# Chunked linear attention inside a long fp32 kernel: scores' full blocks ahead of their corners, the scaling split and moved, a copy on another engine

## The chip, the core and the metric

One core of a Trainium2 chip runs the whole kernel. Its engines take their instructions in order, each from its own queue: TensorE (PE in the profile; its weight loads stand as PEld), VectorE (DVE), ScalarE (ACT), GpSimd (POOL) and SyncE (SP, which issues DMAs). They wait for each other by semaphores. The metric is the device time of one execution in microseconds; lower is better.

## The reference

One block of a model: two gated feed-forward parts around a mixer, on 512 positions of width 1024, in fp32. The change touches the mixer's chunked linear attention, four heads of key width 128 and value width 256, in chunks of 64 positions.

```
b = jnp.cumsum(gc, axis=3)
q_ref = qc * jnp.exp(b - b_ref)
k_ref = kc * jnp.exp(b_ref - b)
scores = jnp.where(causal, jnp.einsum('bhnid,bhnjd->bhnij', q_ref, k_ref), 0.0)
o_intra = jnp.einsum('bhnij,bhnjv->bhniv', scores, vc)
q_inter = q_ref * jnp.exp(b_ref)
k_state = kc * jnp.exp(b_last - b)
kv = jnp.einsum('bhncd,bhncv->nbhdv', k_state, vc)
def step(state, inp):
    dec, kv_n = inp
    return state * dec[..., None] + kv_n, state
o = o_intra + o_inter
```

## The kernel before

**Projections.** Weights come by DMA in fp32. Each is split into a high half `wh` (a cast on ScalarE, L391) and a low half `wl` (a subtraction on VectorE, L392), and each product is taken as three matmuls: high by high, high by low of the activations, low by high. The three buffers of `wh` and of `wl` let this run two units ahead of TensorE. Most projections go by a scheme of seven products (steps m1, p2, q6, p5, q7, p3, p4). The projections v, ga and gb (`Tall`, matmuls at L702) have two halves to each step, 12 matmuls a half; in "ga, p4, second half" the second half of the weights is meant. The ones behind them (`Set`, L586) are numbered from 0 and take 24 matmuls a step. A finished step is evacuated by ScalarE (L1353) or VectorE (L1355). Some sums of weights are made by DMAs of GpSimd's queue that add into a buffer (L360), and by VectorE (L370, L385).

**Attention.** The four heads are worked between the steps of these projections. A table (`hooks`) names, for each step, the pieces that are recorded right behind it. A scheduler then orders each engine's instructions, mostly as they were recorded. A head goes through these pieces:

- `gates` (L1221 to L1230): one matmul, then an absolute value, an exponential and a logarithm on ScalarE (L1224, L1227, L1228), a sum of two on VectorE (L1229) and the running sum along a chunk (a scan, L1230) into tile E.
- `decays` (L1235 to L1245): two differences on VectorE, five exponentials on ScalarE.
- `scale`: nine multiplications on VectorE, all of line L557 (`mul`). Six make the scaled q and k and the tiles KX, QX and KS that scores and state need; three make QS and d2s, which only state and output need.
- `scores`: for each of four blocks of 128 positions (two chunks) a full block (L1272, weights of 128 columns, 128x128) and a corner (L1273, weights of 64 columns, 64x64), which writes a quarter of that full block's place with other scaling; then a masked copy on VectorE (L1275), and three transposes of KS (L1284), copied by ScalarE (L1285).
- `state`: three matmuls (L1294). The first and second write the two halves of one PSUM bank, the third another bank. The first result is copied to the state tile (L1297, VectorE), the others are added to the decayed state before (L1299).
- `output` and `squares`: the two parts of the result (L1313, L1316), and the sum of squares for its norm.

Two PSUM banks (`aux`) serve these pieces in turn.

Of the kernel before, what the change touches and what calls it, by code (L numbers as in the profile page):

```python
# [27 lines left out]
NTB = S // P  # L28
# [192 lines left out]
def block_kernel(ctx: ExitStack, tc: tile.TileContext, xT, vecs, gf, gup, wgl, wts, out):  # L221
    nc = tc.nc
# [37 lines left out]
    def tile_of(pool, shape, dtype=F32):  # L260
        cnt[0] += 1
        return pools[pool].tile(shape, dtype, tag=pool, name=f"{pool}{cnt[0]}")
# [12 lines left out]
    def AUX():  # L275
        cnt[0] += 1
        return pa.tile([P, S], F32, tag="aux", name=f"aux{cnt[0]}")
# [189 lines left out]
    def split(v):  # L467
        h = T(F32R)
        l = T(F32R)
        nc.scalar.copy(h, v)  # L470
        nc.vector.tensor_tensor(out=l, in0=v, in1=h.bitcast(F32), op=ALU.subtract)
        return h, l
# [83 lines left out]
    def mul(out_, a, b, eng=None):  # L556
        (eng or nc.vector).tensor_tensor(out=out_, in0=a, in1=b, op=ALU.mult)  # L557
# [533 lines left out]
    def mixer(norm, nxt):  # L1091
# [15 lines left out]
        def two(i):  # L1107
            return flat(i).rearrange("p (e t) -> p e t", e=2)

        QK = [two(0), two(1)] + [tile_of("qk", [P, 2, S]) for _ in range(2)]  # L1110
# [95 lines left out]
        def pairs(t):  # L1206
            return t.rearrange("p (b e t) -> p b e t", e=2, t=CH)
# [5 lines left out]
        sm4 = sm.rearrange("p a (b e) -> p a b e", e=2)  # L1213
        d2s = cpool.tile([P, NTB], F32, tag="d2", name="d2")
        ST = [M[:, :DV], M[:, DV:], stt2]
        vs = cpool.tile([P, 16 * HEADS], F32, tag="vs", name="vs")

        def gates(h):

            a = AUX()  # L1220
            nc.tensor.matmul(a, gup_w[:R3, h * DK : (h + 1) * DK], glr[:R3],  # L1221
                             start=True, stop=True)
            b = vec[:, V_GB + h : V_GB + h + 1]
            nc.scalar.activation(E, a, AF.Abs, bias=b)  # L1224
            nc.vector.tensor_scalar(out=M, in0=a, scalar1=b, scalar2=0.0,
                                    op0=ALU.add, op1=ALU.min)
            nc.scalar.activation(E, E, AF.Exp, scale=-1.0)  # L1227
            nc.scalar.activation(E, E, AF.Ln, bias=1.0)  # L1228
            nc.vector.tensor_tensor(out=M, in0=M, in1=E, op=ALU.subtract)  # L1229
            nc.vector.tensor_tensor_scan(out=E, data0=reset, data1=M, initial=0.0,  # L1230
                                         op0=ALU.mult, op1=ALU.add)
# [15 lines left out]
        def bc(t):  # L1247
            return t.unsqueeze(2).to_broadcast([P, NTB, CH])

        def scale(h):  # L1250

            q_, k_ = QK[h][:, 0], QK[h][:, 1]
            ref, dc = sm4[:, 0], sm4[:, 1]
            mul(q_, EX, q_)
            mul(KX, pairs(KS)[:, :, 0], pairs(k_)[:, :, 0])
            mul(QX, pairs(q_)[:, :, 1], bc(ref[:, :, 1]))
            mul(pairs(KS)[:, :, 1], pairs(KS)[:, :, 1], pairs(k_)[:, :, 1])
            mul(k_, M, k_)  # L1260
            mul(pairs(KS)[:, :, 0], KX, bc(dc[:, :, 1]))
            mul(pairs(QS)[:, :, 1], QX, bc(dc[:, :, 0]))
            mul(pairs(QS)[:, :, 0], pairs(q_)[:, :, 0], bc(ref[:, :, 0]))
            mul(d2s, dc[:, :, 0], dc[:, :, 1])

        def scores(h):

            q_, k_ = QK[h][:, 0], QK[h][:, 1]
            st = AUX()
            for t in range(NTB):  # L1270
                b = slice(t * P, (t + 1) * P)
                nc.tensor.matmul(st[:, b], k_[:, b], q_[:, b], start=True, stop=True)  # L1272
                nc.tensor.matmul(st[:CH, t * P + CH : (t + 1) * P], KX[:, t], QX[:, t],  # L1273
                                 start=True, stop=True)
            nc.vector.copy_predicated(  # L1275
                sc.rearrange("p (b i) -> p b i", i=P),
                mask.unsqueeze(1).to_broadcast([P, NTB, P]),
                st.rearrange("p (b i) -> p b i", i=P),
            )
            n = NTB - 1  # L1280
            tr = AUX()
            for t in range(n):
                b = slice(t * P, (t + 1) * P)
                nc.tensor.transpose(tr[:, b], KS[:, b], ident)  # L1284
            nc.scalar.copy(E[:, : n * P], tr[:, : n * P])  # L1285

        def state(h):

            v = vt[h // 2]
            for t in range(NTB - 1):  # L1290
                if t % 2 == 0:
                    kv = AUX()
                hc = slice((t % 2) * DV, (t % 2) * DV + DV)
                nc.tensor.matmul(kv[:, hc], E[:, t * P : (t + 1) * P],  # L1294
                                 v[t][:, (h % 2) * DV : (h % 2) * DV + DV], start=True, stop=True)
                if t == 0:
                    nc.vector.tensor_copy(ST[0], kv[:, hc])  # L1297
                else:
                    nc.vector.scalar_tensor_tensor(out=ST[t], in0=ST[t - 1],  # L1299
                                                   scalar=d2s[:, t : t + 1], in1=kv[:, hc],  # L1300
                                                   op0=ALU.mult, op1=ALU.add)
# [3 lines left out]
        def output(h):  # L1305

            v = vt[h // 2]
            for e in range(2):
                o = AUX()
                vc = (h % 2) * DV + e * P  # L1310
                for t in range(NTB):
                    b = slice(t * P, (t + 1) * P)
                    nc.tensor.matmul(o[:, b], v[t][:, vc : vc + P], sc[:, b],  # L1313
                                     start=True, stop=t == 0)
                    if t > 0:
                        nc.tensor.matmul(o[:, b], ST[t - 1][:, e * P : (e + 1) * P],  # L1316
                                         QS[:, b], start=False, stop=True)
                j = 2 * h + e
                nc.scalar.activation(O[h][:, e], o, AF.Copy,
                                     scale=vec[:, V_GLA + j : V_GLA + j + 1])  # L1320
                nc.scalar.activation((E, KS)[e], o, AF.Square)
            nc.vector.tensor_tensor(out=E, in0=E, in1=KS, op=ALU.add)

        def squares(h):

            sh, sl = split(E)
            st = AUX()
            nc.tensor.matmul(st, ones_r, sh, start=True, stop=False)
            nc.tensor.matmul(st, ones_r, sl, start=False, stop=True)
            nc.vector.transpose(E, st)  # L1330
            nc.vector.tensor_scalar(
                out=vs[:, 16 * h : 16 * (h + 1)],
                in0=E.rearrange("p (b c) -> p b c", c=32)[:, :, 0],
                scalar1=1.0 / DV, scalar2=EPS, op0=ALU.mult, op1=ALU.add)
# [81 lines left out]
        def split_o(h):  # L1416
# [3 lines left out]

        hooks = {
            ("v", 0, "q6"): [decays], ("v", 1, "p5"): [lambda: scale(0)],
            ("v", 1, "p3"): [lambda: scores(0)],
            ("ga", 1, "m1"): [lambda: state(0)], ("ga", 1, "p2"): [lambda: output(0)],
            ("ga", 0, "p5"): [lambda: squares(0)], ("ga", 0, "q7"): [lambda: gates(1)],
            ("ga", 1, "q7"): [decays], ("ga", 1, "p3"): [lambda: scale(1)],
            ("gb", 0, "m1"): [lambda: scores(1)], ("gb", 0, "p2"): [lambda: state(1)],
            ("gb", 1, "q6"): [lambda: output(1)], ("gb", 1, "q7"): [lambda: squares(1)],
            ("gb", 0, "p3"): [move], ("gb", 1, "p3"): [lambda: gates(2)],
            ("gb", 0, "p4"): [decays], (0, "q6"): [lambda: scale(2)],  # L1430
            (0, "p3"): [lambda: scores(2)], (1, "q6"): [lambda: state(2)],
            (1, "q7"): [lambda: output(2)], (1, "p3"): [lambda: squares(2)],
            (2, "q6"): [lambda: gates(3)], (2, "q7"): [decays], (2, "p3"): [lambda: scale(3)],
            (3, "q6"): [lambda: scores(3)], (3, "p3"): [lambda: state(3)],
            (4, "q6"): [lambda: output(3)], (4, "p3"): [lambda: squares(3)],
            (5, "q7"): [lambda: normalise(0)], (5, "p3"): [lambda: normalise(1)],
# [201 lines left out]
    with phase("small2", f=10, tp=6, v=4, qk=2, g=1, y=1, small=1):  # L1638
        W.phase(4, 5)
        n2 = Norm(V_G2)  # L1640
        mixer(nm, n2)
# [46 lines left out]
```

## Time and profile before

| | us |
|---|---|
| median of three runs | 1183.71 (1182.52 to 1183.85) |
| the profiled execution | 1182.63 |
| its span (first to last instruction) | 1180.9 |
| ScalarE and VectorE busy | 634.1 and 881.5 |
| mixer's steps with attention | about 380 to 660 of the span |

Times in the profile count from the span's start. In the timeline a row has the start, the time until the end of the last of its instructions, the engine, the line, the operation with the tiles it writes and reads, how many instructions were merged, and in brackets how long the engine was idle before and what ended it. A matmul's end is modelled and overlaps the next one's start, so the distance of starts is what one takes. An fp32 matmul gives two records, an fp32r matmul and a transpose one. The granted clock of TensorE was 0.998 throughout.

### The profile page before, as it was taken

What the parts mean: (1) busy time and instruction counts of PE and PEld (TensorE: products, weight loads), DVE (VectorE), ACT (ScalarE), POOL (GpSimd) and SP (SyncE); (2) the same over time, 40 slices, a digit from 0 to 9 for tenths busy, and PEclk for the clock granted to TensorE, in tenths of its full rate; (3) what the DMA queues carried; (4) which work ended last, traced back from release to release, by engine and by line L of the source; (5) the groups of instructions that cost most, each with busy time, mean ns of one, the idle gap of its engine ahead of it and who ended that gap; (6) DMA issues with size and microseconds to landing.
All of it is one profiled execution on the core that took longest, in us unless ns stands there. A gap on an engine that the chain in (4) does not pass through costs nothing.

```text
span 1180.9 us, 16438 instructions
## 1 busy us (share of the span) xinstructions
PE 1170.5 (99%) x6434; PEld 1018.9 (86%) x6434; DVE 881.5 (75%) x1064; ACT 634.1 (54%) x798; POOL 116.7 (10%) x155
## 2 busy tenths in 40 slices
PE   9999999999999999999999999999999999999997
PEld 8888888999988888789999998888888888898886
DVE  7985667879887966777787999556598565675676
ACT  6555555635362847474655576434355555572353
POOL 0101110011120010111010111000010111000100
PEclk9999999999999999999999999999999999999999
DMA  9677696656474585777566787702656778553431
GB/s 363 132 185 166 157 228 166 173 119 167 117 274 137 109 212 169 206 188 197 134 163 161 177 206 229 274 22 87 212 127 185 169 165 212 147 167 117 90 91 71
DMA packets 58141, 196.92 MB, mean 167 GB/s; under 512 B 6768, under 2 KB 6896, under 8 KB 58064
## 3 DMA queue, kind: packets, MB, share of 16 engines
q1 hardware_dynamic: 36912, 124.27, 31.9%
q0 software_dynamic: 18560, 67.12, 29.8%
q10 hardware_dynamic: 2592, 4.49, 1.0%
q8 instruction: 50, 0.82, 0.3%
q14 instruction: 27, 0.22, 0.1%
HBM read 124.55 MB, written 8.39 MB: 113 GB/s over the span
## 4 chain that ended last, share of the span: by engine, by line
PE 93%; DVE 2%; DMA 2%; issue 1%; ACT 1%; POOL 0%; POOLq 0%; DVEq 0%; ACTq 0%
PE mm L702 37%; PE mm L586 20%; PE mm L443 7%; PE mm L1022 3%; PE mm L419 3%; PE mm L421 3%; PE mm L420 3%; PE mm L972 2%; PE mm L973 2%; PE mm L971 2%; PE mm L462 1%; PE mm L461 1%; PE mm L460 1%; DMA f<-f 1%; PE aux L825 1%
## 5 line engine op out<-in xcount | busy, mean ns | idle before, releaser
L391 ACT CAST wh<-f 128x1024 fp32r<-128x1024 f32 (+1 forms) x337 | 353.2, 1049 | 390.3 <-PE mm L702 124.0
L392 DVE TENSOR_TENSOR wl<-f,wh 128x1024 fp32r<-128x1024 f32 (+1 forms) x337 | 409.7, 1219 | 199.0 <-ACT wh L391 192.2
L702 PE MATMUL mm<-wh,op 128*128 128x512 f32 x1344 | 422.9, 391 | 0.0
L702 PEld LDWEIGHTS mm<-wh,op 128*128 128x128 f32 x1344 | 252.4, 188 | 51.8
L586 PE MATMUL mm<-op,wh 128*128 128x256 f32 x1568 | 284.6, 284 | 0.2 <-ACT tp L591 0.2
L702 PE MATMUL mm<-wl,op 128*128 128x512 f32 x672 | 262.2, 390 | 0.7 <-DVE wl L392 0.7
L586 PEld LDWEIGHTS mm<-op,wh 128*128 128x128 f32 x1568 | 244.6, 191 | 1.3 <-ACT tp L591 0.4
L586 PE MATMUL mm<-op,wl 128*128 128x256 f32 x784 | 222.2, 283 | 0.6 <-DVE wl L392 0.6
L360 POOL DMA_DIRECT2D f<-f x120 | 103.7, 864 | 942.6 <-DVE wl L392 344.9
L586 PEld LDWEIGHTS mm<-op,wl 128*128 128x128 f32 x784 | 149.9, 191 | 0.8 <-DVE wl L392 0.8
L702 PEld LDWEIGHTS mm<-wl,op 128*128 128x128 f32 x672 | 126.3, 188 | 26.1 <-DVE wl L392 0.9
L443 PE MATMUL mm<-op,wh 128*128 128x512 f32 x256 | 64.0, 391 | 0.0
L419 PE MATMUL mm<-op,wh 128*128 128x512 f32 x164 | 63.8, 389 | 0.0
L420 PE MATMUL mm<-op,wh 128*128 128x512 f32 x164 | 63.8, 389 | 0.0
L421 PE MATMUL mm<-op,wl 128*128 128x512 f32 x164 | 63.8, 389 | 0.0
L443 PEld LDWEIGHTS mm<-op,wh 128*128 128x128 f32 x256 | 48.0, 189 | 10.2
L675 DVE TENSOR_TENSOR op<-hid,op 128x1024 fp32r<-128x1024 f32 x35 | 42.7, 1221 | 15.4 <-ACT op L674 15.4
L674 ACT CAST op<-hid 128x1024 fp32r<-128x1024 f32 x35 | 36.6, 1049 | 26.7 <-PE aux L972 20.7
L421 PEld LDWEIGHTS mm<-op,wl 128*128 128x128 f32 x164 | 30.8, 188 | 6.4
L420 PEld LDWEIGHTS mm<-op,wh 128*128 128x128 f32 x164 | 30.8, 188 | 6.4
L419 PEld LDWEIGHTS mm<-op,wh 128*128 128x128 f32 x164 | 30.8, 188 | 6.4
L1022 PE MATMUL mm<-wh,op 128*128 128x512 f32 x112 | 34.6, 389 | 0.0
(288 smaller groups left out, 1350.3 us busy)
## 6 DMA issues: line engine op xcount, KB each, us to landing
f<-wts SPq DMA_DIRECT2D x219, 512.0 KB, 4.3
f<-f POOLq DMA_DIRECT2D x120, 512.0 KB, 5.0
X<-xT SPq DMA_DIRECT2D x8, 256.0 KB, 5.1
xs<-X POOLq DMA_DIRECT2D x8, 256.0 KB, 5.8
ga<-tp ACTq DMA_DIRECT2D x8, 256.0 KB, 3.8
gb<-tp ACTq DMA_DIRECT2D x8, 256.0 KB, 4.4
tp<-ga SPq DMA_DIRECT2D x8, 256.0 KB, 4.9
X<-xs POOLq DMA_DIRECT2D x8, 256.0 KB, 7.5
```

The source lines that it names most:

```text
L360: nc.gpsimd.dma_start(out_, a, accum_op=ALU.add)
L391: nc.scalar.copy(h[:, :w], raw[:, :w])
L392: nc.vector.tensor_tensor(out=l[:, :w], in0=raw[:, :w], in1=h[:, :w].bitcast(F32), op=ALU.subtract)
L419: nc.tensor.matmul(o, wh, ah, start=first, stop=False)
L420: nc.tensor.matmul(o, wh, al, start=False, stop=False)
L421: nc.tensor.matmul(o, wl, ah, start=False, stop=last)
L443: nc.tensor.matmul(o[c], w[:, s : s + P], a[k], start=k == 0 and j == 0, stop=k == kt - 1 and j == 2)
L586: nc.tensor.matmul(to, ww[:, s], aa[:, t], start=fresh and k == 0 and e == 0 and j == 0, stop=k == 3 and j == 2, skip_group_check=True)
L674: nc.scalar.copy(hv, v)
L675: nc.vector.tensor_tensor(out=lv, in0=v, in1=hv.bitcast(F32), op=ALU.subtract)
L702: nc.tensor.matmul(self.bank[b][e], aa[:, c], ww, start=fresh and i == 0 and n == 0, stop=k == 3 and n == 2, skip_group_check=True)
L1022: nc.tensor.matmul(to, aa[:, c], ww, start=fresh and k == 0 and n == 0, stop=k == 3 and n == 2, skip_group_check=True)
```

## The change

In `scores` the four full blocks come first, then the four corners. In `scale` the last three multiplications become a function of their own, `scale_q`, which gets its own places in the table. `gates` and `decays` of head 1 and `scale` of heads 1 and 3 come at other steps. The copy of the first state tile goes from VectorE to ScalarE.

```diff
             mul(pairs(KS)[:, :, 0], KX, bc(dc[:, :, 1]))
+
+        def scale_q(h):
+
+            q_ = QK[h][:, 0]
+            ref, dc = sm4[:, 0], sm4[:, 1]
             mul(pairs(QS)[:, :, 1], QX, bc(dc[:, :, 0]))
             mul(pairs(QS)[:, :, 0], pairs(q_)[:, :, 0], bc(ref[:, :, 0]))
             mul(d2s, dc[:, :, 0], dc[:, :, 1])
...
                 nc.tensor.matmul(st[:, b], k_[:, b], q_[:, b], start=True, stop=True)
+            for t in range(NTB):
                 nc.tensor.matmul(st[:CH, t * P + CH : (t + 1) * P], KX[:, t], QX[:, t],
                                  start=True, stop=True)
...
-                    nc.vector.tensor_copy(ST[0], kv[:, hc])
+                    nc.scalar.copy(ST[0], kv[:, hc])
...
-            ("v", 1, "p3"): [lambda: scores(0)],
+            ("v", 1, "p3"): [lambda: scores(0), lambda: scale_q(0)],
...
-            ("ga", 0, "p5"): [lambda: squares(0)], ("ga", 0, "q7"): [lambda: gates(1)],
-            ("ga", 1, "q7"): [decays], ("ga", 1, "p3"): [lambda: scale(1)],
+            ("ga", 0, "p5"): [lambda: squares(0)], ("ga", 1, "p5"): [lambda: gates(1)],
+            ("ga", 0, "q7"): [decays], ("ga", 0, "p3"): [lambda: scale(1)],
+            ("ga", 0, "p4"): [lambda: scale_q(1)],
...
+            (0, "q7"): [lambda: scale_q(2)],
...
-            (2, "q6"): [lambda: gates(3)], (2, "q7"): [decays], (2, "p3"): [lambda: scale(3)],
+            (2, "q6"): [lambda: gates(3)], (2, "q7"): [decays], (2, "p4"): [lambda: scale(3)],
+            (2, "p3"): [lambda: scale_q(3)],
```

Lines behind `scale` stand 5 to 9 higher in the changed kernel: L1272 and L1273 become L1277 and L1279, L1284 becomes L1290, L1294 L1300, L1297 L1303, L1353 and L1355 L1359 and L1361.

**TensorE at the scores of head 0**, behind the projection v. `mm` is a bank of the projection, `aux` the bank of the scores, `y` holds q and k, `g` tiles of the attention. Before:

```order
L702 MATMUL mm_3752<-wh_3826,op_3799 128x512
L1272 MATMUL aux_3892<-y_3224 128x128
L1273 MATMUL aux_3892<-g_539_3457 64x64
L1272 MATMUL aux_3892<-y_3224 128x128
L1273 MATMUL aux_3892<-g_539_3457 64x64
L1272 MATMUL aux_3892<-y_3224 128x128
L1273 MATMUL aux_3892<-g_539_3457 64x64
L1272 MATMUL aux_3892<-y_3224 128x128
L1273 MATMUL aux_3892<-g_539_3457 64x64
L1284 MATMUL aux_3902<-ident,g_538_3456 128x128 x3
```

Now:

```order
L702 MATMUL mm_3752<-wl_3824,op_3795 128x512
L702 MATMUL mm_3752<-wh_3823,op_3796 128x512
L1277 MATMUL aux_3889<-y_3224 128x128 x4
L1279 MATMUL aux_3889<-g_539_3457 64x64 x4
L1290 MATMUL aux_3899<-ident,g_538_3456 128x128 x3
```

The shapes change twice instead of eight times. It is the same in heads 2 and 3; in head 1 the block stood in two pieces around ten matmuls of gb's m1, and is now in one piece behind all twelve of that half.

**VectorE at the scaling of head 1**, between the steps of ga and gb. Before, `wl_4202` and `wl_4219` belong to the two halves of ga's p4, `wl_4248` to the first half of gb's m1:

```order
L392 TENSOR_TENSOR wl_4219<-f_3855,wh_4218 128x1024
L1355 SCALAR_TENSOR_TENSOR tp_4083<-mm_4087,tp_4083 128x512
L1355 SCALAR_TENSOR_TENSOR tp_4085<-mm_4088,tp_4085 128x512
L557 TENSOR_TENSOR y_3224<-g_539_3457,y_3224 128x512
L557 TENSOR_TENSOR g_538_3456<-g_538_3456,y_3224 128x4x64
L557 TENSOR_TENSOR g_539_3457<-g_538_3456,y_3224 128x256
L557 TENSOR_TENSOR g_539_3457<-y_3224,sm 128x256
L557 TENSOR_TENSOR y_3224<-g_537_3455,y_3224 128x512
L557 TENSOR_TENSOR g_538_3456<-g_539_3457,sm 128x4x64
L557 TENSOR_TENSOR g_540_3458<-g_539_3457,sm 128x4x64
L557 TENSOR_TENSOR g_540_3458<-y_3224,sm 128x4x64
...
L392 TENSOR_TENSOR wl_4248<-f_4136,wh_4247 128x1024
```

Now, with `wl_4202` and `wl_4225` for ga's p4 and `wl_4245` for gb's m1:

```order
L392 TENSOR_TENSOR wl_4202<-f_3805,wh_4201 128x1024
L557 TENSOR_TENSOR y_3224<-g_539_3457,y_3224 128x512
L557 TENSOR_TENSOR g_538_3456<-g_538_3456,y_3224 128x4x64
L557 TENSOR_TENSOR g_539_3457<-g_538_3456,y_3224 128x256
L557 TENSOR_TENSOR g_539_3457<-y_3224,sm 128x256
L557 TENSOR_TENSOR y_3224<-g_537_3455,y_3224 128x512
L557 TENSOR_TENSOR g_538_3456<-g_539_3457,sm 128x4x64
L392 TENSOR_TENSOR wl_4225<-f_3852,wh_4224 128x1024
L1361 SCALAR_TENSOR_TENSOR tp_4083<-mm_4087,tp_4083 128x512
L1361 SCALAR_TENSOR_TENSOR tp_4085<-mm_4088,tp_4085 128x512
L392 TENSOR_TENSOR wl_4245<-f_4144,wh_4244 128x1024
```

The six multiplications of `scale` moved from ahead of gb's first `wl` to ahead of p4's second; the two of QS stand behind gb's first `wl`. Ahead of these rows, the scan and the two differences come after one `wl` of p3 fewer than before, since gates and decays are a step earlier. On ScalarE, L1224 now stands behind the evacuation of p5 and ahead of both casts for p3, and one of these casts between L1224 and L1227.

**VectorE at the scaling of head 3**, in the sets behind gb. `wl_5426` is for the step that runs just ahead of the scores (before; `wl_5432` after), and L370 a sum of weights for a later set. Before:

```order
L1477 SCALAR_TENSOR_TENSOR y_3224<-mm_5102,tp_5195 128x2x256
L370 TENSOR_TENSOR f_5422<-f_5313,f_5317 128x1024
L392 TENSOR_TENSOR wl_5426<-f_5041,wh_5425 128x1024
L1471 TENSOR_TENSOR tp_5453<-mm_5421,tp_5390 128x512
L557 TENSOR_TENSOR qk_3226<-g_539_3457,qk_3226 128x512
L392 TENSOR_TENSOR wl_5456<-f_5045,wh_5455 128x1024
```

Now:

```order
L1486 SCALAR_TENSOR_TENSOR y_3224<-mm_5102,tp_5195 128x2x256
L557 TENSOR_TENSOR qk_3226<-g_539_3457,qk_3226 128x512
L557 TENSOR_TENSOR g_538_3456<-g_538_3456,qk_3226 128x4x64
L557 TENSOR_TENSOR g_539_3457<-g_538_3456,qk_3226 128x256
L557 TENSOR_TENSOR g_539_3457<-qk_3226,sm 128x256
L557 TENSOR_TENSOR qk_3226<-g_537_3455,qk_3226 128x512
L557 TENSOR_TENSOR g_538_3456<-g_539_3457,sm 128x4x64
L370 TENSOR_TENSOR f_5428<-f_5313,f_5317 128x1024
L392 TENSOR_TENSOR wl_5432<-f_5041,wh_5431 128x1024
```

All six multiplications moved ahead of L370 and of that `wl`; before, the first stood behind them and the other five behind the next `wl`, among other rows.

The copy of the first state tile stands on ScalarE behind the cast (L391) that is recorded ahead of it in heads 1 and 3, and behind an evacuation in heads 0 and 2; the second matmul of the state stands behind three matmuls of the projection in head 1 (four before), eight in head 2 (two before), and where it stood in heads 0 and 3.

## The prediction

> **What bounds the kernel now.** First the page's busy times, then the table of waits of TensorE (PE), then the timeline where the changed code runs.
>
> ```profile
> PE 1170.5 (99%) x6434; PEld 1018.9 (86%) x6434; DVE 881.5 (75%) x1064; ACT 634.1 (54%) x798; POOL 116.7 (10%) x155
> ```
>
> TensorE is busy 99% of the span of 1180.9 us: what the other engines do counts only where TensorE waits for it. The change can give time back in two ways: fewer waits, or the same matmuls in less time.
>
> ```profile
> PE mm L702 <- DVE wl L392: 0.7, 1, 0.7
> PE mm L586 <- DVE wl L392: 0.6, 1, 0.6
> PE aux L1294 <- DVE g L1297: 0.6, 1, 0.6
> PE aux L1272 <- DVE qk L557: 0.5, 1, 0.5
> ```
>
> These are the waits of the attention part (us in total, times, longest), 2.4 us in all. The change touches the first, third and fourth. The second lies behind the gates of head 3, whose rows on VectorE (DVE) and ScalarE (ACT) stand as before; it stays.
>
> More is hidden in "busy". This is PE at the scores of head 0 (start us, us, ...; one fp32 matmul gives two records):
>
> ```profile
> 423.50 0.38 PE L1272 MATMUL aux<-y 128*128 128x128 f32 x2
> 423.81 0.33 PE L1273 MATMUL aux<-g 128*64 128x64 f32 x2
> 424.07 0.49 PE L1272 MATMUL aux<-y 128*128 128x128 f32 x2
> 424.49 0.33 PE L1273 MATMUL aux<-g 128*64 128x64 f32 x2
> ...
> 426.10 0.55 PE L1284 MATMUL aux<-ident,g 128*128 128x128 f32 x3
> ```
>
> A full block takes 424.49 - 424.07 = 0.42 us, a corner 424.07 - 423.81 = 0.26, four pairs 426.10 - 423.50 = 2.60. Full blocks of the same shape elsewhere, back to back (output of head 0):
>
> ```profile
> 444.77 0.39 PE L1316 MATMUL aux<-g,g 128*128 128x128 f32 x2
> 445.00 0.39 PE L1313 MATMUL aux<-sc,y 128*128 128x128 f32 x2
> ```
>
> There one takes 0.223 us (0.112 a record). So the alternation of 128-column and 64-column weights costs: after each change of shape the weight load starts only once the matmul before has run out.
>
> **Part 1, corners after full blocks.** Eight shape changes per head become two. From the rows of head 0: the first full block's records start at 423.50 and, with weights loaded ahead, one each 0.112; eight records, so the last starts at +0.78. The corner behind a full block starts 0.20 after that one's last record (423.50 + 0.11 to 423.81): +0.98. A corner that follows a corner is shown nowhere. Its weight loads:
>
> ```profile
> L1273 PEld LDWEIGHTS aux<-g x32: 132/134/136, 423.8 to 605.5; 128*64 128x64 f32 x32
> 424.49 0.19 PEld L1273 LDWEIGHTS aux<-g 128*64 128x64 f32 x2
> ```
>
> Two loads of 0.134 end within 0.19: 0.056 apart, half of a full block's 0.112, as 64 columns are half of 128. I take 0.056 a record. The first corner still has its records 0.11 apart, the other six follow at 0.056: the last starts at 0.98 + 0.11 + 6 x 0.056 = +1.43, and the transposes 0.15 behind it, as the full block at 424.07 is behind the corner's second record (423.81 + 0.11): +1.58 for 2.60. **1.02 us a head.** Bounds: corners at a full block's pitch give 0.69, corners that each still run out (0.26) give 0.58. In head 1 the same pieces are cut in two by ten matmuls of a projection: 2.60 and two restarts of 0.1 (an unprepared full block takes 0.42, the one at 423.50 took 0.31), 2.80; it becomes one block: 1.22. Sum for four heads 4.28, lower bounds 2.96 and 2.52.
>
> [...]
>
> **Part 2, head 1: gates, decays and scaling one to two steps earlier.** A step of a gate projection is 12 matmuls of 0.227 us; its second matmul is the first that needs the low half `wl`, which L392 on VectorE makes.
>
> ```profile
> 470.31 0.39 PE L702 MATMUL mm<-wl,op 128*128 128x512 f32 x1
> 473.03 0.39 PE L702 MATMUL mm<-wl,op 128*128 128x512 f32 x1
> 476.55 0.49 PE L1272 MATMUL aux<-y 128*128 128x128 f32 x2
> 477.71 0.50 PE L702 MATMUL mm<-wl,op 128*128 128x512 f32 x1 [0.67 <-DVE wl L392]
> ```
>
> So `wl` of ga's p4 is due at 470.31 (first half) and 473.03 (second); that of gb's m1 was late by 0.74 (matmul at 477.71, due at 476.97 behind two full blocks and a corner).
>
> ```profile
> 459.65 1.04 ACT L391 CAST wh<-f 128x1024 fp32r<-128x1024 f32 x1
> 462.83 0.69 ACT L1224 ACTIVATE g<-aux,vec 128x512 f32<-128x512 f32 x1
> 466.15 0.69 DVE L1229 TENSOR_TENSOR g<-g,g 128x512 f32<-128x512 f32 x1 [0.71 <-ACT g L1228]
> 467.37 1.21 DVE L1230 TENSOR_TENSOR_SCAN g<-reset,g 128x512 f32<-128x512 f32 x1
> 468.50 1.20 DVE L392 TENSOR_TENSOR wl<-f,wh 128x1024 fp32r<-128x1024 f32 x1
> 469.61 0.68 DVE L1235 TENSOR_TENSOR g<-g 128x512 f32<-128x512 f32 x1
> 471.95 1.28 DVE L1355 SCALAR_TENSOR_TENSOR tp<-mm,tp 128x512 f32<-128x512 f32 x2
> 473.15 0.68 DVE L557 TENSOR_TENSOR y<-g,y 128x512 f32<-128x512 f32 x1
> 475.36 0.75 DVE L557 TENSOR_TENSOR g<-g,sm 128x256 f32<-128x256 f32 x2
> 476.44 2.35 DVE L392 TENSOR_TENSOR wl<-f,wh 128x1024 fp32r<-128x1024 f32 x2
> ```
>
> L1224 now stands right behind the evacuation of p5, where this cast stood: 459.65. L1229 came 3.32 behind L1224; the cast now stands between (+1.0): 463.96, so 2.2 us earlier than before. From there VectorE's row, by the distances of starts above: L1229 0.61, scan 1.13, `wl` 1.11, two differences 1.21, two L1361 (L1355 before) 1.20: `wl` of p4's first half runs 469.22 to 470.44, due 470.31. With a restart, 0.28 lost. Then the six multiplications of `scale` (473.15 to half of the row at 475.36: 2.55), now **ahead** of p4's second `wl`: 470.36 + 2.55 = 472.91, done 474.13, due 473.03 + 0.28. Lost 0.84 and 0.11. Sum 1.23 where 0.74 was lost (its restart is in the 0.20 above): **-0.49**. The multiplications used to stand ahead of gb's first `wl`; the wait goes one step forward and does not vanish, though VectorE idles some 1.4 us before 463.96, since the next row waits for ScalarE. gb's `wl` (475.23 to 476.45) is then in time, and the rest of the scaling stands behind it. Bounds: chain 1.2 us quicker, +0.74; 2.2 us later (as before the move), -2.7.
>
> **Part 3, first state tile by ScalarE.** The second of the state's matmuls writes the bank that this copy reads, and waits for it.
>
> ```profile
> 489.01 0.63 PE L702 MATMUL mm<-wh,op 128*128 128x512 f32 x2
> 490.19 0.70 PE L1294 MATMUL aux<-y,g 128*128 128x256 f32 x2 [0.55 <-DVE g L1297]
> 487.88 1.05 ACT L391 CAST wh<-f 128x1024 fp32r<-128x1024 f32 x1 [1.19 <-PE mm L702]
> 489.72 0.42 DVE L1297 COPY g<-aux 128x256 f32<-128x256 f32 x1
> L1285 ACT COPY g<-aux 128x384 f32<-128x384 f32 x4 | 1.9, 481 | 6.5 <-PE aux L1284 6.5
> ```
>
> In head 1 the copy stood behind VectorE's long rows. On ScalarE it stands behind the cast: 488.84. No copy of 256 is shown there; L1285 takes 0.48 for 384, so 0.37 is my estimate (0.32 to 0.48), done 489.21. The matmul now stands behind three of the projection's matmuls, due 489.24: nearly no wait. **0.65 won**. Head 0 I take as even. In head 3 it is worse:
>
> ```profile
> 623.08 1.05 ACT L391 CAST wh<-f 128x1024 fp32r<-128x1024 f32 x1 [1.83 <-PE mm L586]
> 624.34 0.64 PE L1294 MATMUL aux<-v,g 128*128 128x256 f32 x2
> ```
>
> The copy would run 624.04 to 624.41 behind that cast, the matmul is due 624.34: 0.1 and a restart, -0.2; head 2 between nothing and that, -0.1. Sum **+0.35**. The casts behind it come 0.37 later and wait for a free buffer anyway.
>
> **Part 4, head 3.** `scale(3)` now stands whole ahead of L370 and the next `wl`.
>
> ```profile
> 594.51 0.68 DVE L1477 SCALAR_TENSOR_TENSOR y<-mm,tp 128x512 f32<-128x512 f32 x1
> 596.24 1.22 DVE L392 TENSOR_TENSOR wl<-f,wh 128x1024 fp32r<-128x1024 f32 x1
> 599.37 0.28 PE L586 MATMUL mm<-op,wl 128*128 128x256 f32 x1
> 602.99 0.49 PE L1272 MATMUL aux<-qk 128*128 128x128 f32 x2 [0.47 <-DVE qk L557]
> ```
>
> The scores lost 0.62 and a restart of 0.11: 0.73, gone. But this `wl`, due 599.37, starts 2.55 later, 598.79, and ends 600.02: 0.65 and 0.11. **-0.03**. In heads 0 and 2 the split only shifts rows that nothing waits for.
>
> **Sum:** 4.28 - 0.49 + 0.35 - 0.03 = 4.1 us. All of it lies on TensorE's chain, and behind it nothing else is near the limit, so it passes to the end. The profiled execution took 1182.63 (span 1180.9 and 1.7 around it): 1178.5. That execution lies 1.1 below the median of 1183.71; carried over to the median, **1179.6**.
>
> **Rivals.**
> - *Corners don't stream* (pitch 0.112, or each runs out): 2.8 or 2.35 won, 1180.9 to 1181.4. For it: no pair of corners in the trace. Against: their loads lie 0.056 apart. 20%.
> - *The row on VectorE is worse*: the chain behind L1224 ends 1 to 2.2 us later, p4 waits that much longer: about 2 won, 1181.7. For it: a cast stands in the chain. Against: nothing shows it waiting at 459.65. 10%.
> - *The scaling is hidden*, as its new place would have it: neither p4 nor head 3 waits, 2.0 more: 1177.6. Needs 1.2 us that I don't find. 7%.
> - *Weights aren't loaded ahead within one shape*: full blocks stay at 0.42, corners at 0.26; parts 2 to 4 alone, 1183.9, no change. The rows at 444.77 and 445.00 speak against it. 3%. [...]
> - *Slower*: that cast, now between L1224 and L1227, needs a sum that GpSimd's DMA brings. Each us that it lands after 460.3 is a us on p4. From 4.1 us late the gain is gone, from 6.5 on it is slower by 0.2% (at 7 us late 1186.6). Before, the cast started at once. 5%.
>
> **How the numbers follow.** Forecast 55%. Measurement tells 0.2% (2.4 us) from no change: faster means below 1181.3. That holds the forecast, the hidden case and somewhat under half of the first rival: 0.70. Same: the rest of it, the second, the fourth: 0.25. Slower 0.05. The range: from the hidden case, 1177.5, to the second rival with the runs' spread of some 0.6, 1182.3.
>
> **What would show it.** Right: four L1277 0.22 apart, four L1279 0.11 apart, transposes 1.58 behind the first block; PE waits for `wl` of ga's p4 once more, about 0.8, and none at gb's m1; no wait for the copy in head 1; a wait for `wl` near 599 instead of one at the scores of head 3. Wrong: corners still 0.26 apart, or PE waits in the attention above 3 us.

## The result, and the profile after

The changed kernel takes 1179.72 us (median of 7 runs, 1179.24 to 1180.69) beside 1183.32 for the kernel before on the same chip (7 runs, 1182.52 to 1184.45): ratio 0.997, 95% interval 0.9958 to 0.9982, so 0.3% faster. The profiled execution took 1180.69, the longest of its seven, with a span of 1179.0 at a granted clock of 0.999.

The page's busy times, then TensorE's (PE) table of waits, of the changed kernel:

```profile
PE 1167.7 (99%) x6434; PEld 1017.0 (86%) x6434; DVE 879.7 (75%) x1060; ACT 634.4 (54%) x802; POOL 116.6 (10%) x155
```

```profile
PE mm L586 <- DVE wl L392: 1.1, 2, 0.6
PE aux L286 <- POOL ones L283: 1.1, 1, 1.1
PE mm L586 <- ACT tp L591: 0.8, 1, 0.8
PE mm L461 <- DVE wl L392: 0.8, 1, 0.8
PE mm L702 <- DVE wl L392: 0.7, 1, 0.7
```

The waits for the state's copy (L1294 before) and at the scores (L1272 before) are gone. L586 waits for `wl` twice instead of once; L702 waits as long as before, but at another place. The wait of L461 is new, and lies far behind the attention.

PE at the scores of head 0 and of head 1 (timeline; the distance of starts is what one takes):

```profile
423.72 1.05 PE L1277 MATMUL aux<-y 128*128 128x128 f32 x8
424.70 0.68 PE L1279 MATMUL aux<-g 128*64 128x64 f32 x8
425.31 0.55 PE L1290 MATMUL aux<-ident,g 128*128 128x128 f32 x3
...
478.73 1.05 PE L1277 MATMUL aux<-y 128*128 128x128 f32 x8
479.71 0.68 PE L1279 MATMUL aux<-g 128*64 128x64 f32 x8
480.32 0.55 PE L1290 MATMUL aux<-ident,g 128*128 128x128 f32 x3
```

From the first full block to the transposes it is 425.31 - 423.72 = 1.59 us, where it was 2.60. The four corners take 0.61 with the change of shape behind them, where one alone took 0.26; head 1's block, in one piece now, takes 480.32 - 478.73 = 1.59 too.

The other places that the change touches: head 1's weights of ga's p4, its state, its copy on ScalarE, and head 3's weights.

```profile
473.34 0.50 PE L702 MATMUL mm<-wl,op 128*128 128x512 f32 x1 [0.66 <-DVE wl L392]
487.49 0.40 PE L702 MATMUL mm<-wh,op 128*128 128x512 f32 x1
487.81 0.70 PE L1300 MATMUL aux<-y,g 128*128 128x256 f32 x2
487.39 0.36 ACT L1303 COPY g<-aux 128x256 f32<-128x256 f32 x1
596.98 0.38 PE L586 MATMUL mm<-op,wl 128*128 128x256 f32 x1 [0.54 <-DVE wl L392]
```

The small state matmul stands 0.32 behind the matmul of 0.23 ahead of it; it stood 0.95 behind (489.24 to 490.19, of which 489.01 to 489.24 is one matmul of the row). The wait for `wl` has moved from gb's m1 to ga's p4 in head 1, and head 3's from the scores to the weight cast ahead of them.

How far TensorE is ahead is read from the same matmul in both traces. The first row is of the kernel before, the second of the changed one, behind the last piece of state:

```profile
632.00 0.28 PE L586 MATMUL mm<-op,wl 128*128 128x256 f32 x1
```

```profile
628.14 0.28 PE L586 MATMUL mm<-op,wl 128*128 128x256 f32 x1
```

That is 3.86 earlier, and at the first full block of head 0 it was 0.22 later (423.50 and 423.72): the attention has given **4.08 us**. At the end TensorE is only 1.9 us ahead, the difference of the spans. What is missing, 1.91 us, went in two waits, near 694 us (L586 for ScalarE's L591, 0.76 where it was 0.20) and near 739 us:

```profile
739.65 0.50 PE L461 MATMUL mm<-wl,op 128*128 128x512 f32 x1 [0.76 <-DVE wl L392]
```

The kernel before has no wait at the second place. Whether these two belong to the change was the first open question; the second, which part of the change earns what.

### The profile page after: what moved, and what is told of

Its sections match the earlier page's. It is cut to its first block, busy times and chain, and to the rows that moved or that the text cites. A ratio compares the mean times of both kernels' runs of the same rounds, so it can differ in the third digit from the quotient of the medians.

```text
span 1179.0 us, 16445 instructions
## 1 busy us (share of the span) xinstructions
PE 1167.7 (99%) x6434; PEld 1017.0 (86%) x6434; DVE 879.7 (75%) x1060; ACT 634.4 (54%) x802; POOL 116.6 (10%) x155
## 4 chain that ended last, share of the span: by engine, by line
PE 93%; DVE 3%; DMA 2%; issue 1%; ACT 1%; SPq 0%; POOL 0%; DVEq 0%; ACTq 0%; POOLq 0%
PE mm L702 35%; PE mm L586 22%; PE mm L443 7%; PE mm L1022 3%; PE mm L420 3%; PE mm L421 3%; PE mm L419 3%; PE mm L972 2%; PE mm L973 2%; PE mm L971 2%; DVE wl L392 1%; PE mm L461 1%; PE mm L462 1%; PE mm L460 1%; PE aux L825 1%
## 5 line engine op out<-in xcount | busy, mean ns | idle before, releaser
L391 ACT CAST wh<-f 128x1024 fp32r<-128x1024 f32 (+1 forms) x337 | 353.0, 1048 | 394.2 <-PE mm L702 124.0
L702 PE MATMUL mm<-wh,op 128*128 128x512 f32 x1344 | 423.2, 391 | 0.0
L702 PEld LDWEIGHTS mm<-wh,op 128*128 128x128 f32 x1344 | 252.4, 188 | 51.7
L586 PE MATMUL mm<-op,wh 128*128 128x256 f32 x1568 | 284.6, 284 | 0.8 <-ACT tp L591 0.8
L702 PE MATMUL mm<-wl,op 128*128 128x512 f32 x672 | 262.1, 390 | 0.7 <-DVE wl L392 0.7
L586 PEld LDWEIGHTS mm<-op,wh 128*128 128x128 f32 x1568 | 244.6, 191 | 1.9 <-ACT tp L591 1.0
L586 PE MATMUL mm<-op,wl 128*128 128x256 f32 x784 | 222.2, 283 | 1.1 <-DVE wl L392 1.1
L586 PEld LDWEIGHTS mm<-op,wl 128*128 128x128 f32 x784 | 149.9, 191 | 1.6 <-DVE wl L392 1.5
L702 PEld LDWEIGHTS mm<-wl,op 128*128 128x128 f32 x672 | 126.3, 188 | 26.8 <-DVE wl L392 1.5
L385 DVE TENSOR_TENSOR f<-f,f 128x1024 f32<-128x1024 f32 x24 | 29.3, 1221 | 8.0 <-DMA f<-f 6.1
```

Of the source, the lines that this page charges most:

```text
L391: nc.scalar.copy(h[:, :w], raw[:, :w])
L586: nc.tensor.matmul(to, ww[:, s], aa[:, t], start=fresh and k == 0 and e == 0 and j == 0, stop=k == 3 and j == 2, skip_group_check=True)
L702: nc.tensor.matmul(self.bank[b][e], aa[:, c], ww, start=fresh and i == 0 and n == 0, stop=k == 3 and n == 2, skip_group_check=True)
```

## The experiments

All results in one table. "Attention" is by how much the distance from head 0's first full block to the matmul at 632 us differs from the kernel before, worked out from starts in the two traces as above; "late" is the same from 690 to 745 us. Minus is sooner. Both come from a single trace of each kernel. Three of the rows have the same instructions (changed, changed again, changed with X moved); they differ by 0.3 us in the attention and by 1.8 us in the late stretch.

| kernel | median us | before | ratio, 95% interval | attention | late |
|---|---|---|---|---|---|
| changed | 1179.72 | 1183.32 | 0.9970 (0.9958 to 0.9982) | -4.08 | +1.91 |
| changed, again | 1180.38 | 1183.01 | 0.9973 (0.9963 to 0.9983) | -3.96 | +1.50 |
| corners only | 1179.88 | 1183.01 | 0.9974 (0.9964 to 0.9983) | -3.32 | +0.19 |
| copy only | 1182.45 | 1183.01 | 0.9998 (0.9989 to 1.0006) | -0.42 | 0.0 |
| moved steps only | 1185.94 | 1183.01 | 1.0021 (1.0013 to 1.0030) | +3.53 | 0.0 |
| corners and copy | 1179.23 | 1182.87 | 0.9968 (0.9955 to 0.9980) | -4.30 | +0.51 |
| moved steps and copy | 1183.97 | 1182.87 | 1.0008 (0.9999 to 1.0016) | -0.14 | +1.32 |
| later scaling | 1177.80 | 1182.87 | 0.9951 (0.9939 to 0.9964) | -5.75 | +1.19 |
| later scaling, X moved in the program | 1177.07 | 1183.14 | 0.9948 (0.9935 to 0.9960) | -6.24 | +1.01 |
| changed, X moved in the program | 1179.94 | 1183.14 | 0.9973 (0.9962 to 0.9984) | -4.26 | +0.11 |
| later scaling, X on SyncE | 1176.48 | 1183.33 | 0.9944 (0.9931 to 0.9958) | -6.25 | 0.0 |

Two more have one timed execution each, beside 1182.72 for the kernel before: lagged corners 1181.85, wide corners 1180.71. The wide corners leave the corners' own scores out, so that the output is another; only the times are read.

### The corners only

```diff
             for t in range(NTB):
                 nc.tensor.matmul(st[:, b], k_[:, b], q_[:, b], start=True, stop=True)
+            for t in range(NTB):
                 nc.tensor.matmul(st[:CH, t * P + CH : (t + 1) * P], KX[:, t], QX[:, t],
```

> The kernel before with one edit: the four full blocks of a head's scores first, then their four corners. Theory (each change between 128 and 64 weight columns costs TensorE time): the blocks fall from 2.60 to 1.59 us in heads 0, 2 and 3 and by about as much in head 1, together about 4.2 us, so about 0.35% faster than before, ratio near 0.9965, nearly the whole gain of the change. Rival (the gain comes from the moved steps, the order of the scores only shifts the wait to the next one): under 1 us, ratio above 0.999.

The corners carry most of it, but 0.9 us less in the attention than I expected. Heads 0, 2 and 3 gave 1.0 each. In head 1 two waits grew. VectorE's and TensorE's rows there, with the wait at the gate block first:

```profile
476.92 0.50 PE L702 MATMUL mm<-wl,op 128*128 128x512 f32 x1 [0.90 <-DVE wl L392]
489.16 0.70 PE L1295 MATMUL aux<-y,g 128*128 128x256 f32 x2 [1.09 <-DVE g L1298]
```

```profile
487.55 1.23 DVE L385 TENSOR_TENSOR f<-f,f 128x1024 f32<-128x1024 f32 x1 [1.17 <-DMA f<-f]
488.69 0.42 DVE L1298 COPY g<-aux 128x256 f32<-128x256 f32 x1
```

The state's copy (L1298) was not held up by its own input. It stood behind L385, which waited 1.17 us for weights that GpSimd's queue adds up by DMA. TensorE came 1.6 us sooner there, that sum only 1.0 (488.58 to 487.55), and so the wait for the copy grew from 0.55 to 1.09.

### The copy only

```diff
-                    nc.vector.tensor_copy(ST[0], kv[:, hc])
+                    nc.scalar.copy(ST[0], kv[:, hc])
```

> The kernel before with one edit: the first state tile is copied by ScalarE in all heads. Theory (ScalarE's copy of 0.37 us leaves the two small matmuls behind it no later in sum): between 0.7 us faster and 0.2 us slower, likeliest 0.35 us faster, ratio 0.9997, so within what a measurement can tell. In the trace head 1's wait ahead of the small state matmuls falls from 0.72 to about 0.1 us, and head 2 and head 3 wait 0.1 to 0.3 us more. Rival (ScalarE's copy comes late behind its other work): 0.5 to 1 us slower, with a wait above 0.5 us at those matmuls in head 2 or head 3.

As the theory had it: 0.42 in the trace (0.72 won in head 1, 0.11 and 0.17 lost in heads 2 and 3), not to be told from nothing in the time.

### The moved steps only

The scaling in two parts and the new places of the changed kernel's table, with the order of the scores and the copy as before.

> The changed kernel with the old order of the scores and the old copy on VectorE: only the scaling in two parts and the moved steps are left. Theory (the moved steps only trade one wait for another: 0.74 us at head 1's gate block goes, 1.2 us at head 1's later weight casts comes; 0.73 us at head 3's scores goes, as much comes at the next weight cast): 0.2 to 0.8 us slower than before, ratio 1.0002 to 1.0007. Rival (the moved steps carry part of the gain): 1 to 2 us faster, ratio 0.9985 or less.

Both fell: it is slower, by 0.2%, and in the profiled execution by 3.5 us in the attention. VectorE, TensorE and the windows at head 1's state (the last columns of a window are the granted clock, the DMA share and GB/s):

```profile
490.32 1.23 DVE L385 TENSOR_TENSOR f<-f,f 128x1024 f32<-128x1024 f32 x1 [2.24 <-DMA f<-f]
491.46 0.42 DVE L1302 COPY g<-aux 128x256 f32<-128x256 f32 x1
```

```profile
491.93 0.70 PE L1299 MATMUL aux<-y,g 128*128 128x256 f32 x2 [2.17 <-DVE g L1302]
```

```profile
core 0: us, PE busy (x) PEld busy (x) DVE busy (x) ACT busy (x) POOL busy (x), PEclk, DMA share, GB/s
490.00:492.00 2.00, 0.07 (x1) 0.07 (x1) 1.68 (x3) 0.00 (x0) 0.00 (x0) 1.00 1.08 207
492.00:494.00 2.00, 2.00 (x8) 1.63 (x9) 2.00 (x3) 0.00 (x0) 0.00 (x0) 0.83 0.19 35
494.00:496.00 2.00, 2.00 (x6) 1.53 (x5) 2.00 (x4) 0.61 (x1) 0.00 (x0) 0.50 0.00 0
496.00:498.00 2.00, 2.00 (x9) 1.65 (x8) 1.36 (x2) 0.43 (x1) 0.00 (x0) 0.82 0.68 262
498.00:500.00 2.00, 2.00 (x11) 1.65 (x10) 0.04 (x1) 1.05 (x1) 0.00 (x0) 1.00 0.55 145
```

The copy stands behind the same sum, which now waits 2.24 us. The wait costs 1.6 us more than before. Then TensorE's granted clock falls to 0.50: from 494 to 496 it gets through 6 matmuls instead of about 10. The clocks that are missing, 0.17, 0.50 and 0.18 of 2 us each, make 1.7 us. A wait that the change's other part removes is thus dearer than it looks in the kernel before.

### Corners and copy, without the moved steps; and the moved steps with the copy

> The kernel before with the new order of the scores and the copy of the first state tile on ScalarE; all steps at their old places. With the corners alone, TensorE waited 1.26 us ahead of head 1's small state matmuls (0.72 in the kernel before), because VectorE's copy stood behind a sum that waited for a transfer. Theory (the moved steps bring nothing of their own, the copy takes this wait away): TensorE stands 4.0 to 4.4 us earlier than before at 609 us (3.1 with the corners alone), and the time is 1 us lower than with the corners alone or, where a late transfer makes TensorE wait near 738 us, the same; ratio 0.9955 to 0.9975. Rival (the moved steps are needed for the gain): 3.3 us or less at 609 us.

> The changed kernel with the old order of the scores: moved steps and ScalarE's copy. With the moved steps alone, VectorE's copy stood behind a sum that waited for a late transfer, TensorE waited 2.3 us, and its granted clock fell to 0.50 for about 3.3 us, together 3.2 us later at 500 us. Theory (the copy on ScalarE takes the wait away, and the drop of the clock with it): TensorE stands within 0.6 us of before at 500 us, no stretch at a clock under 0.9 there, ratio 0.9990 to 1.0005. Rival (the moved steps themselves cost the time, the clock falls for another reason): 1.5 to 3 us slower than before, ratio 1.0013 or more, and the clock falls near 493 us again.

Both theories held in the trace. With the copy on ScalarE, head 1's state has no wait above 0.2 us in either, and the granted clock stays at 1.00 in every window from 484 to 500 us. The corners and the copy together give 4.30 in the attention, the whole change 4.08: the moved steps bring nothing that these traces show. The sums of the parts do not add up, since the copy is worth 0.42 beside the kernel before, 0.98 beside the corners (4.30 - 3.32) and 3.67 beside the moved steps (3.53 + 0.14). The steps with the copy take 0.1% more time, with an interval that still holds no change; their trace loses 1.32 us in the late stretch, which the attention does not explain.

### The changed kernel again

> The changed kernel again. About 3.6 us faster than before, ratio 0.997. The profiled execution is looked at for the two late waits (at about 693 and 738 us) that took back 1.9 of the 4.3 us in the first one: if they belong to that execution, they are not there or at another place, and TensorE stands about 4 us earlier than before at the end; if the change makes them, they come back at the same places with 0.6 and 1.2 us.

The two waits came back, at 739 us as long as before (1.03 us over the distance of starts). By the expectation's rule the change would make them. But they also came with the moved steps and the copy, where TensorE stood 0.5 us *later* ahead of the second wait than in the kernel before, and the second did not come with the corners alone, where it stood 3 us earlier. The rule was too simple. The first wait was not followed up: L591 stands on ScalarE behind a cast that waits 2.97 us for a transfer of weight sums (`f<-f`), 2.40 in the kernel before.

### What sets the corners' price: lagged and wide corners

In the first, the corner of a block stands behind the next block; in the second, the corner takes the 128 columns of the keys as weights and moves 64 columns.

```diff
# lagged
-                nc.tensor.matmul(st[:CH, t * P + CH : (t + 1) * P], KX[:, t], QX[:, t],
-                                 start=True, stop=True)
+                for c in ((), (0,), (1,), (2, 3))[t]:
+                    nc.tensor.matmul(st[:CH, c * P + CH : (c + 1) * P], KX[:, c], QX[:, c],
+                                     start=True, stop=True)
# wide
-                nc.tensor.matmul(st[:CH, t * P + CH : (t + 1) * P], KX[:, t], QX[:, t],
+                nc.tensor.matmul(st[:, t * P + CH : (t + 1) * P], k_[:, b], QX[:, t],
```

> The kernel before with the corner of each block issued behind the next block: block 0, block 1, corner 0, block 2, corner 1, block 3, corners 2 and 3. No corner stands right behind its own block, but six of the eight changes between 128 and 64 weight columns stay. Theory (the change of shape is what costs, about 0.17 us each): a head's scores take about 2.26 us, with 0.15 to 0.2 us over the pitch at each of the six changes. Rival (the corner waits for the block that has just been written beside it): about 1.6 us, like the order with all blocks first.

> The kernel before, where the corners' matmul takes 128 weight columns (the keys) and moves 64 columns of the queries, still block, corner, block, corner; the corners' scores are left out, so that the output differs. Theory (the number of weight columns is what makes the array run empty): no stall between block and corner, a head's scores at 1.9 us or less. Rival (the size of the moving tile or the place in PSUM makes it): the scores stay near 2.6 us.

PE at head 0's scores with lagged corners:

```profile
423.95 0.60 PE L1272 MATMUL aux<-y 128*128 128x128 f32 x4
424.49 0.33 PE L1274 MATMUL aux<-g 128*64 128x64 f32 x2
424.75 0.49 PE L1272 MATMUL aux<-y 128*128 128x128 f32 x2
425.17 0.33 PE L1274 MATMUL aux<-g 128*64 128x64 f32 x2
...
426.22 0.55 PE L1285 MATMUL aux<-ident,g 128*128 128x128 f32 x3
```

2.27 us with six changes of shape, as worked out; the corner that no longer stands behind its own block takes 0.26 and the block behind it 0.42, exactly as before. With wide corners:

```profile
423.34 0.38 PE L1272 MATMUL aux<-y 128*128 128x128 f32 x2
423.56 0.33 PE L1273 MATMUL aux<-g,y 128*128 128x64 f32 x2
423.73 0.44 PE L1272 MATMUL aux<-y 128*128 128x128 f32 x2
...
425.07 0.50 PE L1284 MATMUL aux<-ident,g 128*128 128x128 f32 x3
```

1.73 us although blocks and corners alternate as in the kernel before: a corner takes 0.17, not 0.26. So it is the change of the weights' columns, not the small moving tile and not the neighbouring place in PSUM. That the array runs empty in between, as the theory words it, no row shows: the rows give only when matmuls and weight loads start. (With the weights' columns the partitions of the result go from 64 to 128, and the weights come from the block's own tile; these were not tested apart.)

### A better place for the scaling

Head 1's scaling goes behind one more weight cast and its second part behind the scores; head 3's decays, scaling and scores go one step later.

```diff
-            ("ga", 0, "q7"): [decays], ("ga", 0, "p3"): [lambda: scale(1)],
-            ("ga", 0, "p4"): [lambda: scale_q(1)],
-            ("gb", 0, "m1"): [lambda: scores(1)], ("gb", 0, "p2"): [lambda: state(1)],
+            ("ga", 0, "q7"): [decays], ("ga", 1, "p3"): [lambda: scale(1)],
+            ("gb", 0, "m1"): [lambda: scores(1), lambda: scale_q(1)], ("gb", 0, "p2"): [lambda: state(1)],
...
-            (2, "q6"): [lambda: gates(3)], (2, "q7"): [decays], (2, "p4"): [lambda: scale(3)],
-            (2, "p3"): [lambda: scale_q(3)],
-            (3, "q6"): [lambda: scores(3)], (3, "p3"): [lambda: state(3)],
+            (2, "q6"): [lambda: gates(3)], (2, "p4"): [decays], (2, "p3"): [lambda: scale(3)],
+            (3, "p5"): [lambda: scores(3), lambda: scale_q(3)], (3, "p3"): [lambda: state(3)],
```

> The changed kernel with head 1's scaling behind one more weight cast (its second part behind the scores) and head 3's decays, scaling and scores one step later. Theory (VectorE's scaling stands ahead of weight casts that TensorE already waits for): the waits of 0.23 and 0.94 us in head 1 and of 0.84 and 0.80 us in head 3 go, and at most 0.85 us comes back at head 1's gate block and 0.5 us in head 3: 1.4 to 2.8 us less in the attention stretch than the changed kernel, TensorE 5.4 to 6.8 us earlier than before at 609 us; the time 1177.5 to 1179.5, where late transfers take some of it back. Rival (VectorE is so full that each wait only moves): as long as the changed kernel, 1179.7 to 1180.4, with new waits of as much at the next casts.

TensorE's waits in it:

```profile
PE mm L461 <- DVE wl L392: 0.8, 1, 0.8
PE aux L1300 <- ACT g L1303: 0.4, 1, 0.4
PE mm L702 <- DVE wl L392: 0.2, 1, 0.2
PE mm L586 <- ACT tp L591: 0.2, 1, 0.2
```

Both waits of L586 for `wl` in head 3 are gone, and L702's in head 1 is 0.23 instead of 0.66; that for the copy, 0.35, is new, and the next kernel, with the same steps, hasn't got it. The attention gives 5.75 us, 1.67 more than the changed kernel, and the time is 5.1 us below the kernel before. The rival's wait for a wait did not come. The wait of L461 stayed.

### The late wait: the loads of X

Near 739 us the weights share the transfer engines with eight loads of X, 2 MB on GpSimd's queue, which nothing reads before 808 us: in the changed kernel, from 726 to 740 us, the queue of the weights and the gate loads takes 56.5% of the 16 engines' time and that of X 43.8%.

```diff
-                if e == 0 and k == 1:
+                if e == 1 and k == 2:
                     XS.append(big("X2"))
```

> The version with the later scaling, and the eight loads of X (256 KB each, first used at 808 us) some 30 us later, where the transfers idle. Theory (from 725 to 745 us the 16 DMA engines are full, and the weights that TensorE needs at 736 us come late behind these 2 MB): the wait of 1.03 us ahead of the first L461 matmul is gone and none of that size comes elsewhere; TensorE stands 5.7 to 6.3 us earlier than before at the end (4.8 without this edit), the time 1176.2 to 1177.3. Rival (the weights come late because of their own queue, the gate loads ahead of them): the wait stays at 0.7 us or more, the time stays at 1177.4 to 1178.2.

> The changed kernel with the eight loads of X some 30 us later. Theory (as for the version with the later scaling): the wait near 738 us (1.03 us in two profiled executions of the changed kernel) is gone, TensorE stands 3.3 to 4.2 us earlier than before at the end, the time 1178.2 to 1179.3. Rival (the queue of the weights itself): the wait stays at 0.7 us or more and the time at 1179.7 to 1180.4.

This edit moved nothing on the chip. GpSimd's queue has no other work there, and the loads start when an operation of VectorE (L1562 with the later scaling) has ended, wherever they stand in the program: at 723.72 us without the edit and at 723.20 with it. On every engine the instructions have the order of the kernel without the edit. The first of these kernels kept the wait (0.73 us). The second is the changed kernel a third time, and it shows what I had got wrong: its profiled execution took 1178.43 us and has no wait at 739, as the theory wanted, but not for the theory's reason. The same instructions run with that wait and without it; it is not a fixed price of the change.

What comes late there is read from ScalarE's rows, first in the kernel before (with TensorE's matmul), then in the changed one, whose matmul stands at 739.65 above:

```profile
738.65 0.63 ACT L1568 ACTIVATE tp<-tp 128x512 f32<-128x512 f32 x1 [3.92 <-DMA tp<-ga]
739.19 1.04 ACT L391 CAST wh<-f 128x1024 fp32r<-128x1024 f32 x1
741.74 0.40 PE L461 MATMUL mm<-wl,op 128*128 128x512 f32 x1
```

```profile
736.77 0.63 ACT L1577 ACTIVATE tp<-tp 128x512 f32<-128x512 f32 x1 [4.99 <-DMA tp<-ga]
737.30 1.04 ACT L391 CAST wh<-f 128x1024 fp32r<-128x1024 f32 x1
```

The cast from which the matmul's `wl` is made stands on ScalarE behind an operation on a gate, and this one waits for a load of ga, 256 KB on SyncE's queue. The cast itself then starts without a wait: not its weights are late, as theory and rival had it, but the gate load ahead of it. From issue to landing that load takes 7.7 us in the kernel before and 9.1 in the changed one. In the kernel before the matmul starts 2.55 us behind the cast (741.74 - 739.19), in the changed one, where it waits, 2.35 (739.65 - 737.30): 0.2 us were to spare. All thirteen traces with X on GpSimd's queue fit this. In the six where the load takes 6.6 to 7.8 us TensorE has no such wait; in the seven where it takes 8.3 to 9.1 it waits 0.20 to 0.76. The execution of 1178.43 us is the one with 6.6.

To move the loads of X for good they went to SyncE's queue, behind the weights:

```diff
-                        nc.gpsimd.dma_start(x[k_], xs[k_])
+                        tc.keep_in_program_order(nc.sync.dma_start(x[k_], xs[k_]))
```

> The version with the later scaling, and the eight loads of X on SyncE's queue, behind the weights that TensorE needs at 736 us (the earlier try only moved them in the program: GpSimd's queue still started them at 723 us). Theory (the weights share the transfer engines with these 2 MB): they land at least 1 us sooner, the wait of 0.9 to 1.03 us ahead of the first L461 matmul is gone, and TensorE stands 5.7 to 6.5 us earlier than before at the end, the time 1176.0 to 1177.0. Rival (it is their own queue with the gate loads): the wait stays at 0.7 us or more, the time at 1177.0 to 1178.0, or later where the loads of X now hold up the next weights.

That gate load (KB, us from issue to landing) and the issue of X, in the version with the later scaling:

```profile
tp<-ga SPq DMA_DIRECT2D x1, 256.0 KB, 9.0
```

```profile
723.72 4.30 POOL L1601 DMA_DIRECT2D X<-xs  x8 [18.03 <-DVE op L1562]
```

And with X on SyncE:

```profile
tp<-ga SPq DMA_DIRECT2D x1, 256.0 KB, 4.2
```

```profile
732.68 5.55 SPq L1601 DMA_DIRECT2D X<-xs  x8
```

The load is issued at about the same time (724.96 and 724.40 us) and lands in 4.2 us, sooner than in any of the thirteen traces with X beside it; ScalarE waits 0.54 us for it where it waited 4.74, TensorE's wait is gone, and TensorE keeps at the end all that the attention gave. In a single trace the wait's absence could be chance, as it was above; the quicker landing speaks for the cause. Theory and rival were each half right: late was a gate load, and X made it late. At 1176.48 us this version has the lowest median, 6.9 us below the kernel before; its runs (1176.06 to 1177.08) overlap with the ten of the same steps with X on GpSimd's queue (1176.40 to 1177.92).

## Why the prediction was right, point by point

The predicted 1179.6 us is 0.1 from the median. Part of this closeness is luck: the 4.1 us were taken from a median of 1183.71, the runs beside the changed kernel have 1183.32, and the gain between the medians is 3.60; the two differences nearly cancel. The profiled execution, for which 1178.5 was worked out, took 1180.69. It is in the attention that the working can be judged. By heads, predicted and measured gain there:

| | head 0 | head 1 | head 2 | head 3 | sum |
|---|---|---|---|---|---|
| predicted | 1.02 | 1.22 - 0.49 + 0.65 = 1.38 | 1.02 - 0.1 = 0.92 | 1.02 - 0.03 - 0.2 = 0.79 | 4.1 |
| measured | 0.99 | 1.40 | 0.91 | 0.78 | 4.08 |

Three traces of the same instructions have 4.08, 3.96 and 4.26 as the sum, so the agreement to 0.02 is closer than traces repeat.

- **Part 1** (1.58 for a head's scores): 1.59. A corner behind a corner takes half of a full block, as the two weight loads had hinted; the rival of corners that don't stream is out. So is the one where weights are not loaded ahead within one shape: eight records of full blocks stand 0.112 apart, and those of corners 0.058 (medians). In the kernel before the load for the matmul at 444.77 starts at 444.66, 0.11 us ahead of it and beside the matmul that starts at 444.66. At a change of shape it starts together with its own matmul, at 423.81 and at 424.07 in head 0. That the matmul ahead has run out by then is my reading: its modelled end, 423.88 and 424.14, lies 0.07 us later. The price goes with the changes of shape, as the lagged and wide corners show: 2.27 us with six changes, 1.73 with none.
- **Part 2** (0.28 and 0.95 lost in head 1): 0.23 and 0.94. The wait moved and did not vanish. (In the working 474.13 - 473.03 - 0.28 gives 0.82, not 0.84, which changes nothing.) The rival in which the cast behind L1224 waits for a sum of GpSimd's DMA did not come: it started at 459.45 us without a wait.
- **Part 3** (0.65 in head 1, small losses in heads 2 and 3): the distance of 0.95 shrank to 0.32 there, 0.63 won; heads 2 and 3 lost 0.11 and 0.17 at the copy, where 0.1 and 0.2 were put. ScalarE's copy took 0.36 to 0.38 us, where I had put 0.37. As an effect beside the kernel before it is right. What I missed is that the copy's price on VectorE hangs on a transfer (L385) and on the other parts: with the copy on VectorE the moved steps cost not 0.5 but 3.5 us.
- **Part 4** (0.73 gone at the scores, 0.76 new at the weights): 0.73 and 0.80.
- **What failed** is the step behind the sum: that behind the attention nothing else is near the limit, so the gain passes to the end. Near 739 us the kernel before had 0.2 us to spare, as shown above, and a gate load that takes 1.4 us longer than there uses it up. One execution lost 1.91 us in the late stretch, another of the same instructions 0.11; that one took 1178.43, and 1178.5 was worked out for the profiled execution. The spread of such executions can account for the half us between the worked 4.1 and the 3.6 between the medians; that was not measured run by run.

What stays open: what decides, from one execution to another, how fast these transfers go. That X slows them was shown in one trace (4.2 us without X beside the load); why the same instructions sometimes get their gate load in 6.6 us and sometimes in 9.1 was not, and neither was what makes the wait near 694 us longer.

## What to carry to other kernels

Sort matmuls by the shape of their weights before looking for anything cleverer: it gave 3.3 of the 4.1 us and needed no other work to change. A small copy between TensorE and a long in-order queue costs what stands ahead of it, and here that was a wait for a transfer, of 1.17 us with the corners only and of 2.24 with the moved steps; measure it in the version that will run, since here it was worth 0.4, 1.0 or 3.7 us. Before moving a step, find the cast or load that TensorE will ask for next, and put the step behind it. Before counting a gain as time at the end, look for the places behind it with little to spare: here 0.2 us of slack at one load took back up to a third of the gain.

## What the runs showed of the hardware

- With the moved steps only, after a wait of 2.2 us, TensorE ran at a granted clock of 0.50 for some 3 us (1.7 us are missing in three windows), which cost as much as the wait's growth; a wait of 1.1 us at the same place, with the corners only, left the clock at 1.00 in the window behind it:

```profile
490.00:492.00 2.00, 2.00 (x11) 1.63 (x10) 2.00 (x4) 0.26 (x1) 0.00 (x0) 1.00 0.00 0
492.00:494.00 2.00, 2.00 (x10) 1.69 (x9) 2.00 (x4) 0.80 (x1) 0.00 (x0) 1.00 0.19 71
```

- Each change between weights of 128 and of 64 columns cost about 0.17 us: a block of four full matmuls and four corners took 2.60 us with eight changes, 2.27 with six and 1.59 with two.
- The loads of X, on a queue that had nothing else to do, started when the operation that they wait for had ended, and not where the program has them: recorded at a later step, they started at 723.20 us instead of 723.72.
- A load of 256 KB landed in 4.2 us without the 2 MB of X in transit beside it, and in 6.6 to 9.1 us with them.
